# Moving work at the joints of one decoder step: page gathers, operand pieces, squares, splits and closing adds in another order

## The chip, the cores and the metric

The kernel runs on one core of a Trainium2 chip. Times are device microseconds of one execution of the whole program; the time of a kernel is the median of several runs. Five engines work side by side, each through its own queue in order: TensorE (PE, with its weight loads PEld), VectorE (DVE), ScalarE (ACT), GpSimd (POOL), and SyncE (SP), which only issues DMA.

## The reference

One decoder layer in float32, for a prompt of 1024 tokens and 8 sampled tokens with 256 cached positions each; model width 1024, feed-forward width 4096.

```python
z = rmsnorm(x, g_mix) @ w_in          # q, k, v, indexer qi/ki/wi, u, vb, ga, gb
score = sum_h relu(qi_h . ki) * wi_h  # indexer: over the prompt, or over gathered cache pages
idx   = top_k(score, min(256, L//4))  # then softmax attention over the kept keys
o_sgu = u * (tril(w_s) rmsnorm(vb) + b_s)
x = x + (sigmoid(ga) * o_att + sigmoid(gb) * o_sgu) @ w_o
x = x + square(relu(rmsnorm(x, g_ffn) @ w_up)) @ w_down
x = x + sigmoid(rmsnorm(x, g_ple) @ w_pg) * (p @ w_p)
```

For the sampled tokens, keys, values and indexer keys come from paged caches through a page table (8 sequences of 2 pages).

## The kernel before, in words

All activations are feature-major: 8 chunks of 128 features by 1032 tokens (1024 + 8). Each float32 product is made of three passes over a high and a low half of each operand (xh,whi; xl,whi; xh,wlo), so every operand needs a cast to the high half on ACT and a subtraction for the low half on DVE or POOL. `split_weight` does that for a weight chunk (ACT: L195 whi, POOL or DVE: L196 wlo). A projection chunk is 72 matmuls, `acc`.

The program is written out by hand in the order of each engine's queue; there is no scheduler that reorders it. Each engine executes what is emitted for it in that order, and semaphores follow from the data. Generators in a list `paced` are advanced one step at each `tick` of the projection loop; the top-k runs as a background generator on DVE. SBUF tiles called `slot` share a ring of 40 buffers.

In order of time: input norm and indexer queries; projections of queries, keys, values, gates and the spatial gating unit (65 to 690 us of the profiled execution), with the top-k on DVE and the decode path between them; attention to 918; the out-projection w_o, chunks k = 0 to 7, to 1015.7; the up-projection to 1372; a first part of the embedding product p @ w_p to 1393; the down-projection to 1737; the second part to about 1752; w_pg to the end.

- `decode` gathers the indexer's cache pages by 16 indirect DMAs on POOL (L652, tile `kib`); between pairs of them POOL copies decode queries into `zqi` (L684).
- The out-projection also prepares the up-projection's right operand: `scale` (L1309), `square` for the norm (L1248), and `x_piece(i, kk)`, which forms a sum or difference of quarters of x for product i (DVE, in place) and splits it (ACT cast L1317, DVE residual, tile `xop`).
- The up-projection is done by a 7-product scheme on 2 by 2 blocks. 16 steps `USTEPS` of 7 products, each product 24 matmuls into PSUM pairs pa, pd, pc, pb. `up_split` makes the weight pieces (`uop`, L1366). Evictions: `Pair.to` copies on ACT (first, L1292) or adds on DVE. The norm's factor `r` is computed by `inv_rms` in the first step (a power on POOL, L276) and spread over the tokens by transposes (`along_banks`, banks rb and rbd, copied by ACT, L1519 and L1522). At a step's end the two halves `top` and `low` go through relu times norm on DVE and are squared on ACT (L1590, L1595); `operands` then emits the pieces for the down-projection in the next step (`hop`, L1421), partly through DRAM.
- The down-projection has 32 steps (8 passes f over the feed-forward blocks, 4 output pairs o) of 7 products of 12 matmuls. Weight pieces: `down_sums` on POOL (`ds`, L1490 to L1493), `down_hi` on ACT (`dhi`, L1500), `down_lo` on DVE (`dlo`). `split_op` splits the raw operands of products 4 to 6, loaded as `hraw` by `load_op`, in the first step of their pass. In the last pass each step ends with adds of u2 into the result (DVE) and two squares for the next norm (ACT, then sums into `acc` on POOL, L1250).

Of the kernel before, what the change touches and what calls it, by code (L numbers as in the profile page):

```python
# [16 lines left out]
P = 128  # L17
D = 1024
S = 1024
NB = 8  # L20
# [50 lines left out]
def step_kernel(ctx, tc, xT, pT, w_in, w_o, w_up, w_down, w_pg, w_p, gv, gqk, wsT, b_s,  # L71
# [355 lines left out]

    at[0] = 2
# [214 lines left out]
    def decode():  # L643
        pt = small("pt", [P, NB * NPG], I32)
        sp.dma_start(out=pt, in_=bass.AP(tensor=pages.tensor, offset=pages.offset, ap=[[0, P], [1, NB * NPG]]))
        io = small("io", [P, 1], I32)
        pool.iota(io, pattern=[[0, 1]], base=0, channel_multiplier=1)
        pf = small("pf", [P, NB * NPG + 1])
        idx = small("idx", [P, NB * NPG], I32)

        def page(out, cache, j):
            pool.indirect_dma_start(out=out, out_offset=None, in_=cache,  # L652
                                    in_offset=bass.IndirectOffsetOnAxis(ap=idx[:, j:j + 1], axis=0))

# [16 lines left out]
        yield 1  # L671
        yield 1
        dve.tensor_copy(pf[:, :NB * NPG], pt)
        dve.tensor_copy(pf[:, NB * NPG:], io)
        dve.tensor_scalar(idx, pf[:, :NB * NPG], float(P), pf[:, NB * NPG:], op0=ALU.mult, op1=ALU.add)
        kib = slot("kib", [P, NB * NPG, HD])
        zqi = slot("zqi", [64, NB, NB, HI])
        pool.memset(zqi, 0.0)
        for j in range(NB * NPG):
            page(kib[:, j, :], cache_ki, j)  # L680
            if j % 2 == 1:
                for h in range(2):
                    b = j // 2
                    pool.tensor_copy(zqi[:, b, b, h::2], dqi[h * 64:(h + 1) * 64, :, b])  # L684
                yield 1
# [628 lines left out]
    def x_keep(i, kk, r, c):  # L1314
        xop[i, kk] = op = slot("xop", [P, 2, TH], F32R)
        src = quarter(kk, r, c)
        act.copy(op[:, 0], src)  # L1317
        dve.tensor_tensor(out=op[:, 1], in0=src, in1=op[:, 0].bitcast(F32), op=ALU.subtract)

# [3 lines left out]
    def x_piece(i, kk):  # L1323
# [10 lines left out]
        x_keep(i, kk, *((0, 0), (0, 0), (1, 0), (1, 1), (0, 1), (1, 1), (1, 0))[i])  # L1334
# [37 lines left out]
    n1 = Norm(2, "1", x1)  # L1372
    for k in range(KC):
# [10 lines left out]
        if k:  # L1384
            if k < KC - 1:
                scale(k - 1)
            if k - 1 < 4:
                x_piece(0, k - 1)
                x_piece(1, k - 1)
            elif k - 1 == 4:  # L1390
                for i in range(2, 7):
                    x_piece(i, 0)
        if k == KC - 2:
            for g in range(LEAD):
                up_split(g)
            up_load(1)
            scale(k)

# [126 lines left out]
    def up_product(n, i, pair, start, between=None):  # L1525
        w = wop.pop(7 * n + i)
        for kk in range(4):
# [3 lines left out]
            for l, r in ((0, 0), (0, 1), (1, 0)):  # L1531
# [4 lines left out]
    FIRST_X = {1: [(2, 1), (2, 2), (2, 3)], 2: [(3, 1), (3, 2), (3, 3), (4, 1)], 3: [(4, 2), (4, 3)],  # L1536
               4: [(5, 1), (5, 2), (5, 3)], 5: [(6, 1), (6, 2), (6, 3)]}

    for n, (f, j) in enumerate(USTEPS):
# [5 lines left out]
        for i in range(7):  # L1545
# [5 lines left out]
            for x in FIRST_X.get(i, ()) if n == 0 else ():  # L1551
                x_piece(*x)
# [14 lines left out]
            if n == 0 and i == 3:  # L1567
# [9 lines left out]
            if i == 0:  # L1577
                t.to(u, True)
            elif i == 1:
                t.to(c22, True)  # L1580
            elif i == 3:
                for p, o, r in tiles["a"].views(c11, n1.R[:, :TH]):
                    dve.scalar_tensor_tensor(out=o, in0=p, scalar=0.0, in1=r, op0=ALU.max, op1=ALU.mult)
            elif i == 4:
# [7 lines left out]
            elif i == 6:  # L1592
                t.plus(c21, u)
                dve.scalar_tensor_tensor(out=low, in0=low, scalar=0.0, in1=n1.R, op0=ALU.max, op1=ALU.mult)
                act.activation(low, low, AF.Square)  # L1595
# [3 lines left out]
    for low_ in lows:  # L1599
        low_()  # L1600

# [57 lines left out]
    for n, (f, o) in enumerate(steps):  # L1659
# [9 lines left out]
        if o == 2:  # L1669
            for i in range(4, 7):  # L1670
                load_op(follows, i)
# [22 lines left out]
        d.to(c22, first)  # L1694
        if end:
# [3 lines left out]
        split_op(f, 4)  # L1699
# [3 lines left out]
        split_op(f, 5)  # L1703
# [29 lines left out]
        if last:  # L1733
            dve.tensor_tensor(out=d12, in0=d12, in1=u2, op=ALU.add)
            both = acc[:, 2 * o + 1, :].rearrange("p (s c) -> p s c", s=2)
            dve.tensor_tensor(out=both, in0=both, in1=u2.unsqueeze(1).to_broadcast([P, 2, TH]), op=ALU.add)
            for k in (o, o + 4):
                n2.square(k)
            if o == 2:
                embed_load(1)  # L1740
    ks = [0, 4, 1, 5, 2, 6, 3, 7]
# [98 lines left out]
```

## Time and profile before

| | us |
|---|---|
| time, median of 3 runs | 1853.52 (1852.42 to 1854.61) |
| profiled execution, its own time | 1852.57 |
| its span | 1850.6 |
| PE busy | 1771.4 (96%) |
| DVE busy | 1385.2 (75%) |
| ACT busy | 754.7 (41%) |
| POOL busy | 582.9 (31%) |

In rows of a timeline the first number is the start, the second the length; what stands in brackets is the idle time of that engine just before, and what ended it. In rows of waits stand the total, the number of waits and the longest. A line L65 is that of a helper that records every operation of PE and DVE, so those are told apart by the names of their tiles.

### The profile page before, as it was taken

Reading aid. Unit: us, or ns where it says so; the run is one execution under the profiler, and the core shown is the slowest. Engines: PE = TensorE matmul, PEld = TensorE weight load, DVE = VectorE, ACT = ScalarE, POOL = GpSimd, SP = SyncE. Lnnn points to the kernel's source line nnn. Section 1 sums busy time; section 2 is a strip of 40 time slices with the busy share of each in tenths; the row PEclk is TensorE's granted clock in tenths of the full one; section 3 lists DMA queues with packets and bytes.
Section 4 is the critical chain, followed back from the end, with each engine's and each line's share of the span. In section 5 each row is a group of like instructions: output and inputs, shape, how many; then the busy total and the mean of one; then the engine's idle time right before and its main releaser. Section 6 shows DMA issues by size and latency. Waiting matters only on the chain. (4 is left out here: it accounts for less than half of the span.)

```text
span 1850.6 us, 31610 instructions
## 1 busy us (share of the span) xinstructions
PE 1771.4 (96%) x12490; PEld 1657.9 (90%) x12490; DVE 1385.2 (75%) x2505; ACT 754.7 (41%) x1304; POOL 582.9 (31%) x479
## 2 busy tenths in 40 slices
PE   8999988999999999999999899999989999999898
PEld 8998887998999996777698799999989999999798
DVE  7489986989978756777734788888884777777733
ACT  5544332255311136777733543444445322222521
POOL 3233354456323221110013133222323335432321
PEclk9999999999999999999999899999999999999999
DMA  4122132223122264223151154554526566653133
GB/s 172 59 96 103 58 122 85 90 94 114 47 92 69 92 166 119 58 63 98 49 195 69 53 203 180 192 182 175 197 104 230 203 220 236 211 176 127 71 113 122
DMA packets 118932, 236.19 MB, mean 128 GB/s; under 512 B 12856, under 2 KB 57792, under 8 KB 118784
## 3 DMA queue, kind: packets, MB, share of 16 engines
q1 hardware_dynamic: 116592, 229.43, 36.7%
q0 software_dynamic: 2048, 4.72, 0.9%
q8 instruction: 98, 1.61, 0.4%
q14 instruction: 50, 0.41, 0.1%
q10 hardware_dynamic: 144, 0.02, 0.0%
HBM read 155.22 MB, written 78.91 MB: 127 GB/s over the span
## 5 line engine op out<-in xcount | busy, mean ns | idle before, releaser
L65 PE MATMUL acc<-xh,whi 128*128 128x344 f32 (+1 forms) x1144 | 372.8, 329 | 2.2 <-DVE s_q L65 1.8
L65 PE MATMUL acc<-xh,wlo 128*128 128x344 f32 (+1 forms) x1144 | 365.2, 323 | 7.9 <-POOL wlo L196 6.4
L65 PE MATMUL acc<-xl,whi 128*128 128x344 f32 (+1 forms) x1144 | 364.9, 322 | 2.1 <-DVE xl L65 2.1
L65 PEld LDWEIGHTS acc<-xh,whi 128*128 128x128 f32 x1144 | 216.3, 190 | 11.1 <-issue 5.0
L65 PEld LDWEIGHTS acc<-xh,wlo 128*128 128x128 f32 x1144 | 215.9, 189 | 9.1 <-POOL wlo L196 7.0
L65 PEld LDWEIGHTS acc<-xl,whi 128*128 128x128 f32 x1144 | 216.0, 189 | 3.6 <-DVE xl L65 3.1
L65 DVE MATCH_REPLACE8 mask<-m,mask 128x384 f32<-128x384 f32 (+2 forms) x192 | 166.6, 875 | 0.0
L196 POOL TENSOR_TENSOR wlo<-wraw,whi 128x1024 fp32r<-128x1024 f32 x47 | 113.5, 2416 | 159.8 <-ACT whi L195 111.2
L65 DVE MAX8 m<-mask 128x8 f32<-128x384 f32 (+2 forms) x192 | 161.0, 879 | 0.0
L1113 ACT ACTIVATE p<-p,mx,s_q 128x1024 f32<-128x1024 f32 (+7 forms) x128 | 110.4, 864 | 24.2 <-DVE mx L65 23.8
L65 PE MATMUL pa<-xop,uop 128*128 128x258 f32 x768 | 101.3, 289 | 10.9 <-ACT x L1292 10.9
L65 PEld LDWEIGHTS pa<-xop,uop 128*128 128x128 f32 x768 | 96.5, 193 | 14.3 <-ACT x L1292 13.8
L65 PE MATMUL pc<-xop,uop 128*128 128x258 f32 x768 | 101.0, 287 | 2.6 <-ACT xop L1317 1.9
L65 PEld LDWEIGHTS pc<-xop,uop 128*128 128x128 f32 x768 | 96.7, 192 | 4.0 <-ACT xop L1317 2.6
L65 DVE CUSTOM_DVE_ANT_0 p<-sc,mask 128x1024 f32<-128x1024 f32 (+5 forms) x96 | 83.5, 886 | 21.2 <-PE sc L65 20.7
L65 PE MATMUL pd<-xop,uop 128*128 128x258 f32 x768 | 99.2, 285 | 0.0
L65 DVE TENSOR_TENSOR x<-x 128x516 f32<-128x516 f32 x92 | 95.7, 1040 | 0.7
L65 PEld LDWEIGHTS pd<-xop,uop 128*128 128x128 f32 x768 | 96.0, 192 | 0.0
L65 PE MATMUL pc<-hop,dhi 128*128 128x258 f32 x512 | 84.8, 286 | 7.6 <-DVE acc L65 7.6
L65 PE MATMUL sc<-kh,qst 128*128 128x512 f32 (+3 forms) x384 | 89.2, 361 | 1.6 <-DVE mx L65 1.4
L1490 POOL TENSOR_TENSOR ds<-draw 128x256 f32<-128x256 f32 x32 | 31.3, 979 | 186.8 <-DMA draw<-w_down 37.6
L65 PE MATMUL pa<-hop,dhi 128*128 128x258 f32 x512 | 83.4, 285 | 3.7 <-DVE u L65 3.6
(339 smaller groups left out, 4132.7 us busy)
## 6 DMA issues: line engine op xcount, KB each, us to landing
h_d<-hop SPq DMA_DIRECT2D x56, 516.0 KB, 3.7
hop<-h_d SPq DMA_DIRECT2D x56, 516.0 KB, 5.7
wraw<-w_in SPq DMA_DIRECT2D x48, 512.0 KB, 4.7
uraw<-w_up SPq DMA_DIRECT2D x32, 512.0 KB, 4.8
draw<-w_down SPq DMA_DIRECT2D x32, 512.0 KB, 3.7
hs_d<-x SPq DMA_DIRECT2D x42, 258.0 KB, 2.8
hraw<-hs_d SPq DMA_DIRECT2D x21, 516.0 KB, 6.4
q_d<-qs SPq DMA_DIRECT2D x16, 512.0 KB, 3.2
```

Of the source, the lines that this page charges most:

```text
L65: return fn(*args, **kw)
L196: eng.tensor_tensor(out=lo, in0=raws[n], in1=hi.bitcast(F32), op=ALU.subtract)
L1113: eng.activation(s, s, AF.Exp, bias=env["mx"][:, 4 + h:5 + h], scale=sc, accum_out=env["sum"][:, h:h + 1])
L1490: pool.tensor_tensor(out=s_[:, 0], in0=a21, in1=a22, op=ALU.add)
```

## The change

It moves operations; each of them is still done once and with the same operands.

- Index pages: the page table's DMA, the index computation and the 16 gathers move from `decode` into a generator `index_pages`, paced through the indexer-query stage. In `decode` only the zqi copies remain.
- Out-projection: pieces go into a list `xq` and are issued two after each eviction of a block, so that a chunk's whi and wlo come ahead of them. Four pieces of products 2 and 3 come into the last chunk.
- First up step: pieces come in batches (`x_pieces`: all sums, then all casts, then all residuals). The transposes of the norm's factor move from product 3 to product 4, and the eviction that uses it from product 3's end to product 4's.
- Up steps: the square of `low` is kept in `squared` and issued after the next step's copy out of pa.
- End of up: the loads for the first embedding come at product 2, its casts at product 4, its residuals at products 4, 5 and 6, and the first sums of down weights at product 6.
- Down: `split_op` of raw operand 4 comes in step o = 2 and of 5 in o = 3 of the pass before, only 6 stays in o = 0; the raw loads come one per step.
- Last pass: the closing adds and squares of a step become `close`, called after product 1 of the next step.

```diff
+    def index_pages():
+        sp.dma_start(out=pt, in_=bass.AP(tensor=pages.tensor, offset=pages.offset, ap=[[0, P], [1, NB * NPG]]))
+        pool.iota(io, pattern=[[0, 1]], base=0, channel_multiplier=1)
+        yield 1
+        dve.tensor_copy(pf[:, :NB * NPG], pt)
+        dve.tensor_copy(pf[:, NB * NPG:], io)
+        dve.tensor_scalar(idx, pf[:, :NB * NPG], float(P), pf[:, NB * NPG:], op0=ALU.mult, op1=ALU.add)
+        yield 1
+        paged["kib"] = kib = slot("kib", [P, NB * NPG, HD])
+        for j in range(NB * NPG):
+            page(kib[:, j, :], cache_ki, j)
+            if j % 2 == 1:
+                yield 1
...
+    paced.append(pages_)
...
-        for j in range(NB * NPG):
-            page(kib[:, j, :], cache_ki, j)
-            if j % 2 == 1:
-                for h in range(2):
-                    b = j // 2
-                    pool.tensor_copy(zqi[:, b, b, h::2], dqi[h * 64:(h + 1) * 64, :, b])
-                yield 1
+        yield 1
+        for b in range(NB):
+            for h in range(2):
+                pool.tensor_copy(zqi[:, b, b, h::2], dqi[h * 64:(h + 1) * 64, :, b])
+            yield 1
...
+    def x_pieces(which):
+
+        for i, kk in which:
+            x_sum(i, kk)
+        for i, kk in which:
+            xop[i, kk] = op = slot("xop", [P, 2, TH], F32R)
+            act.copy(op[:, 0], quarter(kk, *AT[i]))
+        for i, kk in which:
+            less(xop[i, kk][:, 1], quarter(kk, *AT[i]), xop[i, kk][:, 0].bitcast(F32))
...
-        for a, b, p in (in_step(M, W=W0 if k == 0 else None) if k in (0, KC - 1) else dense(M)):
+        blocks = in_step(M, W=W0 if k == 0 else None) if k in (0, KC - 1) else dense(M)
+        while xq and k == KC - 1:
+            x_pieces([xq.pop(0)])
+        for a, b, p in blocks:
             dve.tensor_tensor(out=x1[k][:, a:b], in0=p, in1=x1[k][:, a:b], op=ALU.add)
+            for _ in range(2):
+                if xq and k > 1:
+                    x_pieces([xq.pop(0)])
...
             if k - 1 < 4:
-                x_piece(0, k - 1)
-                x_piece(1, k - 1)
+                xq += [(0, k - 1), (1, k - 1)]
             elif k - 1 == 4:
-                for i in range(2, 7):
-                    x_piece(i, 0)
+                xq += [(i, 0) for i in range(2, 7)]
+            elif k - 1 == 5:
+                xq += [(2, 1), (3, 1)]
         if k == KC - 2:
...
             scale(k)
+            xq += [(2, 2), (3, 2)]
...
-    FIRST_X = {1: [(2, 1), (2, 2), (2, 3)], 2: [(3, 1), (3, 2), (3, 3), (4, 1)], 3: [(4, 2), (4, 3)],
-               4: [(5, 1), (5, 2), (5, 3)], 5: [(6, 1), (6, 2), (6, 3)]}
+    FIRST_X = {1: [(2, 3), (3, 3)], 2: [(4, 1), (4, 2)], 3: [(4, 3), (5, 1)],
+               4: [(5, 2), (5, 3), (6, 1)], 5: [(6, 2), (6, 3)]}
+    squared = []
...
+            if end and i == 2:
+                embed_load(0)
             if end and i == 3:
-                embed_load(0)
                 down_load(0)
                 down_load(1)
-            if end and i == 5:
+            if end and i == 4:
                 lows, first_embed = embed(0)
+            if end and i > 3:
+                lows.pop(0)()
+            if end and i == 6:
                 down_sums(0)
...
-            if n == 0 and i == 3:
+            if n == 0 and i == 4:
                 def between():
                     n1.R = along_banks(n1.r, "R_1")
...
             if i == 0:
                 t.to(u, True)
+                if squared:
+                    x = squared.pop()
+                    act.activation(x, x, AF.Square)
...
-            elif i == 3:
+            if i == (4 if n == 0 else 3):
                 for p, o, r in tiles["a"].views(c11, n1.R[:, :TH]):
...
-                act.activation(low, low, AF.Square)
+                if end:
+                    act.activation(low, low, AF.Square)
+                else:
+                    squared.append(low)
...
-    for low_ in lows:
-        low_()
...
-        if o == 2:
-            for i in range(4, 7):
-                load_op(follows, i)
+        if o:
+            load_op(follows, o + 3)
...
         d.to(c22, first)
+        if last and o:
+            close()
...
-        split_op(f, 4)
         product(n, f, 2, A12, a, False)
         a.to(c11, first)
         free(2)
-        split_op(f, 5)
+        if o > 1:
+            split_op(follows, o + 2)
...
         if last:
-            dve.tensor_tensor(out=d12, in0=d12, in1=u2, op=ALU.add)
...
+            def close(o=o, d12=d12, u2=u2):
+                dve.tensor_tensor(out=d12, in0=d12, in1=u2, op=ALU.add)
...
             if o == 2:
                 embed_load(1)
+    close()
```

Three places show what stands where in a queue. The first is POOL. Before, in the decode path: `kib` are the pages, `zqi` the decode queries, `sg` a gate, `wlo` the low half of a projection's weight.

```order
L652 DMA kib<-cache_ki,idx 128x64 x2
L684 COPY zqi<-dqi 64x4 x2
L839 TENSOR_SCALAR sg<-sg 128x1032
L196 TENSOR_TENSOR wlo<-wraw,whi 128x1024
L652 DMA kib<-cache_ki,idx 128x64 x2
L684 COPY zqi<-dqi 64x4 x2
L481 AFFINE_SELECT mask<-mask 128x128
```

Now, in the indexer-query stage (`r_x` is the input norm's factor, raised to its power on POOL):

```order
L196 TENSOR_TENSOR wlo<-wraw,whi 128x1024
L436 DMA kib<-cache_ki,idx 128x64 x2
L276 TENSOR_TENSOR r_x<-r_x,half 128x9
L436 DMA kib<-cache_ki,idx 128x64 x2
L196 TENSOR_TENSOR wlo<-wraw,whi 128x1024
L436 DMA kib<-cache_ki,idx 128x64 x2
L409 COPY kid<-kis 64x8
L436 DMA kib<-cache_ki,idx 128x64 x2
L196 TENSOR_TENSOR wlo<-wraw,whi 128x1024
L436 DMA kib<-cache_ki,idx 128x64 x6
L196 TENSOR_TENSOR wlo<-wraw,whi 128x1024
L436 DMA kib<-cache_ki,idx 128x64 x2
```

The gathers have left the neighbourhood of the gates' weights and stand among the weights of the indexer's queries.

The second place is ACT at the end of the out-projection, from chunk 6 to chunk 7: `sq` is the norm's square, `xop` the operand pieces, `whi` the high half of chunk 7's weight. Before:

```order
L1248 ACTIVATE sq<-x_9370 128x1032
L1309 ACTIVATE x_9370<-x_9370,gvt 128x1032
L1317 CAST xop<-x_9370 128x516 x5
L195 CAST whi<-wraw 128x1024
L1248 ACTIVATE sq<-x_9370 128x1032
```

Now:

```order
L1259 ACTIVATE sq<-x_9370 128x1032
L1320 ACTIVATE x_9370<-x_9370,gvt 128x1032
L195 CAST whi<-wraw 128x1024
L1334 CAST xop<-x_9370 128x516 x5
L1259 ACTIVATE sq<-x_9370 128x1032
```

The weight's cast has passed the five pieces.

The third is ACT at the joint of two up steps: the squares are the ACTIVATE rows (first the top half, then the low half), the COPY empties pa. Before:

```order
L1590 ACTIVATE x_9370<-x_9370 128x1032
L1366 CAST uop<-uraw 128x512
L1595 ACTIVATE x_9370<-x_9370 128x1032
L1366 CAST uop<-us 128x512
L1292 COPY x_9370<-pa 128x516
```

Now:

```order
L1621 ACTIVATE x_9370<-x_9370 128x1032
L1381 CAST uop<-uraw 128x512
L1381 CAST uop<-us 128x512
L1303 COPY x_9370<-pa 128x516
L1609 ACTIVATE x_9370<-x_9370 128x1032
```

The low half's square has passed a weight cast and the copy.

More of the change, by code (lines that the diff above doesn't have):

```diff
@@ L426, in index_weights, with page @@
                           in1=r2w[:NB, NT:].to_broadcast([NB, HI]), op=ALU.mult)
+    paged = {}
+    pt = small("pt", [P, NB * NPG], I32)
+    io = small("io", [P, 1], I32)
+    pf = small("pf", [P, NB * NPG + 1])
+    idx = small("idx", [P, NB * NPG], I32)
+    def page(out, cache, j):
+        pool.indirect_dma_start(out=out, out_offset=None, in_=cache,
+                                in_offset=bass.IndirectOffsetOnAxis(ap=idx[:, j:j + 1], axis=0))
+    def index_pages():
[11 more added lines that the diff above has]
+                yield 1
+    pages_ = index_pages()
     at[0] = 2
@@ L643, in decode @@
     def decode():
[L644 to L653, printed above, removed]
+        while pages_ in paced:
+            yield 1
         sel = small("sel", [64, NB, HQ])
@@ L670, in decode @@
         sp.dma_start(out=wc, in_=wd.rearrange("b (h o) -> (b h) o", o=1))
-        yield 1
[L672 to L676, printed above, removed]
+        kib = paged["kib"]
         zqi = slot("zqi", [64, NB, NB, HI])
         pool.memset(zqi, 0.0)
-        for j in range(NB * NPG):
-            page(kib[:, j, :], cache_ki, j)
-            if j % 2 == 1:
-                for h in range(2):
-                    b = j // 2
-                    pool.tensor_copy(zqi[:, b, b, h::2], dqi[h * 64:(h + 1) * 64, :, b])
-                yield 1
+        yield 1
+        for b in range(NB):
+            for h in range(2):
+                pool.tensor_copy(zqi[:, b, b, h::2], dqi[h * 64:(h + 1) * 64, :, b])
+            yield 1
         yield 1
@@ L1312, in quarter, with x_sum @@
         return xg[kk + 4 * r][:, c * TH:c * TH + TH]
[L1314 to L1318, printed above, removed]
     def less(out, x, y):
         dve.tensor_tensor(out=out, in0=x, in1=y, op=ALU.subtract)
-    def x_piece(i, kk):
+    def x_pieces(which):
[6 more added lines that the diff above has]
+            less(xop[i, kk][:, 1], quarter(kk, *AT[i]), xop[i, kk][:, 0].bitcast(F32))
+    AT = ((0, 0), (0, 0), (1, 0), (1, 1), (0, 1), (1, 1), (1, 0))
+    def x_sum(i, kk):
         b11, b12, b21, b22 = (quarter(kk, r, c) if i > 1 or not r else None for r in range(2) for c in range(2))
@@ L1333, in x_piece @@
             less(b21, b21, b22)
-        x_keep(i, kk, *((0, 0), (0, 0), (1, 0), (1, 1), (0, 1), (1, 1), (1, 0))[i])
     wraws, wsum, wop = {}, {}, {}
@@ L1372, in step_kernel @@
     n1 = Norm(2, "1", x1)
+    xq = []
     for k in range(KC):
@@ L1550, in step_kernel @@
             up_split(7 * n + i + LEAD)
-            for x in FIRST_X.get(i, ()) if n == 0 else ():
-                x_piece(*x)
+            if n == 0 and i in FIRST_X:
+                x_pieces(FIRST_X[i])
             if i:
@@ L1578, in step_kernel @@
                 t.to(u, True)
+                if squared:
+                    x = squared.pop()
+                    act.activation(x, x, AF.Square)
             elif i == 1:
                 t.to(c22, True)
-            elif i == 3:
+            if i == (4 if n == 0 else 3):
                 for p, o, r in tiles["a"].views(c11, n1.R[:, :TH]):
                     dve.scalar_tensor_tensor(out=o, in0=p, scalar=0.0, in1=r, op0=ALU.max, op1=ALU.mult)
-            elif i == 4:
+            if i == 4:
                 t.to(c22, False)
@@ L1733, in step_kernel @@
         if last:
-            dve.tensor_tensor(out=d12, in0=d12, in1=u2, op=ALU.add)
[L1735 to L1738, printed above, removed]
+            def close(o=o, d12=d12, u2=u2):
+                dve.tensor_tensor(out=d12, in0=d12, in1=u2, op=ALU.add)
+                both = acc[:, 2 * o + 1, :].rearrange("p (s c) -> p s c", s=2)
+                dve.tensor_tensor(out=both, in0=both, in1=u2.unsqueeze(1).to_broadcast([P, 2, TH]), op=ALU.add)
+                for k in (o, o + 4):
+                    n2.square(k)
             if o == 2:
                 embed_load(1)
+    close()
     ks = [0, 4, 1, 5, 2, 6, 3, 7]
```

## The prediction

> **What bounds the kernel now.** I read the page's busy table first, then the waits of TensorE, then the windows of the stages, and then the timeline around each long wait.
>
> ```profile
> span 1850.6 us, 31610 instructions
> PE 1771.4 (96%) x12490; PEld 1657.9 (90%) x12490; DVE 1385.2 (75%) x2505; ACT 754.7 (41%) x1304; POOL 582.9 (31%) x479
> ```
>
> TensorE (PE) is busy for all but 79.2 us. No matmul is added or removed, so the change can win only those idle microseconds, plus what the clock loses after them. The waits of PE over the whole span, as total, times and longest:
>
> ```profile
> PE pa L65 <- ACT x L1292: 10.9, 14, 0.8
> PE pc L65 <- DVE acc L65: 7.6, 8, 1.0
> PE acc L65 <- POOL wlo L196: 6.4, 2, 6.1
> PE acc L65 <- DVE pl L65: 5.3, 1, 5.3
> PE vtr L65 <- ACT rl L470: 4.4, 2, 4.1
> PE rb L65 <- POOL r L276: 4.2, 1, 4.2
> PE pa L65 <- DVE u L65: 3.6, 3, 1.8
> PE acc L65 <- ACT whi L195: 2.9, 1, 2.9
> PE pc L65 <- ACT xop L1317: 1.9, 3, 1.0
> PE acc L65 <- DVE pwlo L65: 1.6, 1, 1.6
> PE pd L65 <- DVE dlo L65: 0.5, 1, 0.5
> ```
>
> Nearly every row is a joint that the diff touches. The windows show the stages: after the length come busy time and instructions of PE, PEld, DVE, ACT and POOL, then the granted clock.
>
> ```profile
> 918.00:992.00 74.00, 74.00 (x471) 74.00 (x472) 31.85 (x41) 25.48 (x29) 14.53 (x7) 1.00 0.42 151
> 1000.36:1015.70 15.34, 14.31 (x72) 13.80 (x73) 5.20 (x8) 4.72 (x6) 4.05 (x3) 0.78 0.30 104
> 1015.70:1050.90 35.20, 28.42 (x191) 25.82 (x190) 25.63 (x42) 16.55 (x29) 8.64 (x5) 0.86 0.12 45
> 1050.90:1350.50 299.60, 289.50 (x2363) 286.80 (x2363) 254.36 (x367) 128.14 (x211) 92.06 (x56) 0.99 0.51 183
> 1350.50:1393.00 42.50, 33.74 (x233) 32.54 (x233) 32.62 (x45) 22.56 (x39) 7.93 (x8) 0.92 0.23 88
> 1393.00:1693.00 300.00, 293.27 (x2408) 290.99 (x2407) 208.90 (x336) 87.45 (x108) 115.24 (x120) 1.00 0.59 207
> 1693.00:1752.00 59.00, 51.63 (x356) 47.16 (x355) 46.57 (x65) 27.29 (x34) 22.52 (x15) 0.97 0.18 65
> 296.00:690.00 394.00, 391.64 (x2555) 378.03 (x2554) 327.50 (x572) 118.12 (x226) 149.91 (x102) 1.00 0.31 95
> 290.80:294.00 3.20, 3.16 (x12) 3.16 (x13) 0.00 (x0) 0.78 (x1) 2.15 (x3) 0.53 0.56 179
> ```
>
> An undisturbed stretch (918 to 992) does 471 instructions in 74.00 us, 0.157 us each. A wait costs twice: itself, and a clock near one half for the next microseconds (last row, right after the 6.1 us wait).
>
> **The change, part by part.** The sum is made against this execution: its own time is 1852.57 us (span 1850.6 and 2.0 around it), 0.95 below the median of 1853.52, which I use as base.
>
> *A, index pages.* Sixteen page gathers and their zqi copies stand in POOL's queue in decode, ahead of a wlo that PE wants:
>
> ```profile
> 278.38 0.18 POOL L684 COPY zqi<-dqi 64x4 f32<-64x4 f32 x1 [3.10 <-DMA kib<-cache_ki,idx]
> 288.44 2.34 POOL L196 TENSOR_TENSOR wlo<-wraw,whi 128x1024 fp32r<-128x1024 f32 x1
> 290.84 0.66 PE L65 MATMUL acc<-xh,wlo 128*128 128x344 f32 x1 [6.14 <-POOL wlo L196]
> ```
>
> A zqi copy waits for a transfer (3.10), and POOL holds everything behind it. With the gathers gone this wlo can start some 10 us earlier (eight zqi pairs and twelve gathers stand in the stretch before it), so the wait goes whole (6.1) and with it the slow clock: 3.2 us at 0.53, half of it lost, 1.5. That is 7.6. The cost lies in the query stage, where the gathers now stand between POOL's operations of 42 to 80 us, with one small DMA more on SP and three small operations on DVE:
>
> ```profile
> L652 POOL DMA_INDIRECT kib<-cache_ki,idx x16 | 18.1, 1129 | 4.9 <-issue 2.8 <-POOL zqi L684 1.8
> 65.05 2.39 POOL L196 TENSOR_TENSOR wlo<-wraw,whi 128x1024 fp32r<-128x1024 f32 x1 [5.33 <-ACT whi L195]
> 77.77 2.40 POOL L196 TENSOR_TENSOR wlo<-wraw,whi 128x1024 fp32r<-128x1024 f32 x1 [10.33 <-ACT whi L195]
> ```
>
> They take 18.1 us in all, 1.13 each. POOL's gaps ahead of its wlo are 5.33 and 10.33 us, filled by waiting for ACT's whi: two to four gathers (2.3 to 4.5) go into the one and six (6.8) into the other, so they cost nothing. If the indices came late, the wlo of these rows would queue behind them. I take 7; bounds 4 (a later wait by VectorE eats some) and 7.6. The vtr wait of 4.1 I leave as it is: ahead of it POOL is held by a power for fk, not by a gather.
>
> *B, end of the out-projection.* On ACT five piece casts, each waiting for a DVE subtraction, stand ahead of the last block's whi:
>
> ```profile
> 998.74 0.62 ACT L1317 CAST xop<-x 128x516 fp32r<-128x516 f32 x1 [1.43 <-DVE x L65]
> 999.27 1.04 ACT L195 CAST whi<-wraw 128x1024 fp32r<-128x1024 f32 x1
> ```
>
> PE waits 2.9 for it (the row from ACT whi); then 72 matmuls take 15.34 us instead of 72 x 0.157 = 11.3, at clock 0.78. With whi ahead both go: 2.9 + 4.0 = 6.9. The pieces now fall into the block itself, where DVE has 5.20 of 15.34 us busy. I take 6.5; bounds 4 and 7.
>
> The Trainium skill ("TensorE: Matmul & The Clock Gate", Part 1) says that the clock halves after at least one idle window of about 3.4 us. This trace shows 0.78 after a wait of 2.9 followed by shorter ones, so the measurement decides here; by the page alone part B would be worth the waits only, about 4, and the whole forecast some 3 us less.
>
> *C, first up step.* It lasts 35.20 us for 191 instructions of PE. In the steps after it one takes 289.50 / 2363 = 0.1225, so 23.4 would do. Waits are 4.2 (rb, for POOL's power) and 1.9 for xop, and most of the rest is the clock at 0.86. DVE works 25.63 of it, and between a piece's subtraction and its residual it idles for ACT's cast:
>
> ```profile
> 1027.52 0.70 DVE L65 TENSOR_TENSOR xop<-x,xop 128x516 fp32r<-128x516 f32 x1 [0.69 <-ACT xop L1317]
> ```
>
> The batches close that 0.69, some twelve times, and four pieces have moved into B. So DVE's 25.6 us become the floor: 35.2 - 25.6 = 9.6 at best. The transposes move one product (24 x 0.1225 = 2.9 us) later, which takes most of the 4.2; but now rbd waits until ACT has copied the first rb, and ACT's queue has the batch's casts of products 4 and 5 ahead of that copy, which wait for DVE. I charge 1.6 for it: gain 8; bounds 4 (the stall as long as the rb wait was) and 9.6.
>
> *D, the square behind the copy.* In each of 14 steps ACT squares the previous step's low half, then casts, then copies u out of pa, for which PE waits:
>
> ```profile
> 1141.30 1.07 ACT L1595 ACTIVATE x<-x 128x1032 f32<-128x1032 f32 x1 [2.70 <-DVE x L65]
> 1142.78 0.58 ACT L1292 COPY x<-pa 128x516 f32<-128x516 f32 x1
> 1143.41 3.15 PE L65 MATMUL pa<-xop,uop 128*128 128x258 f32 x24 [0.75 <-ACT x L1292]
> ```
>
> Behind the copy, the 1.07 us square is after what PE waits for. The copy may start 1 us earlier, more than the 0.75 of the wait. All 10.9 go unless another wait follows in its place; DVE is busy 254 of 299.6 us there, so a little may. I take 10; bounds 7 and 10.9. Who waits for the square is the hop cast of a later product, with ACT 128 of 299.6 busy.
>
> *E, end of up.* Embedding casts and residuals move one product earlier, each residual between products. The 5.3 and 1.6 for pl and pwlo are what can go, and the clock behind them (stage at 0.92); but DVE has 32.62 us of work in 42.50, and pl only moves ahead of work which is late itself, up to the hop pieces that bound the embedding. I take 3; bounds 0 and 6.9.
>
> *F, raw splits.* Of three hop splits in one down step, two move to the step before. Here a 1.23 us split stands just ahead of the eviction for which PE waits:
>
> ```profile
> 1441.50 1.23 DVE L65 TENSOR_TENSOR hop<-hraw,hop 128x1032 fp32r<-128x1032 f32 x1
> 1442.64 0.75 DVE L65 TENSOR_TENSOR acc<-pc,acc 128x258 f32<-128x258 f32 x2
> ```
>
> One such wait of about 0.95 occurs per pass, 7.6 in 8. One split stays in that step; with two gone, DVE's queue is 2.4 us shorter. I take 4.5; bounds 2 and 7. The loads move to one a step on SP, far ahead of their use.
>
> *G, closing adds of the last pass.* They move behind product 1 of the next step, after the pd eviction. This removes the 3.6 for u, the 0.5 for dlo, and some 1.5 of slow clock (as in A). But the squares follow the adds, and POOL's sums of the next step's weight halves stand behind the squares:
>
> ```profile
> 1712.75 4.92 POOL L1250 TENSOR_TENSOR acc<-acc,sq 128x1032 f32<-128x1032 f32 x2 [4.85 <-ACT sq L1248]
> 1717.62 1.47 POOL L1490 TENSOR_TENSOR ds<-draw 128x256 f32<-128x256 f32 x1
> 1719.16 0.74 POOL L1491 TENSOR_TENSOR ds<-ds,draw 128x256 f32<-128x256 f32 x1
> 1721.32 1.05 ACT L1500 CAST dhi<-ds 128x1024 fp32r<-128x1024 f32 x1 [6.78 <-POOL ds L1493]
> ```
>
> Before, this dhi comes just in time for product 1 of the last step. Now the closing adds start two products and an eviction later (2 x 12 x 0.122 + 0.7 = 3.6), and squares, sums and dhi with them. I count dhi 3 us late in the last step and 2 in the one before, where there is more room, dlo 0.8 more in each: 6.6, with 1.5 of slow clock. 5.6 gained against 8.1: I take -2; bounds -5 (four more sums of 0.74 that take twice as long, as one does above) and +3 (dhi late by half of that).
>
> The Trainium skill ("GPSIMD Engine Reference", Key points) says that GpSimd shares its SBUF interfaces with VectorE, with contention when a DVE instruction has two SBUF inputs. The trace agrees: one ds sum took 1.47 and the next 0.74. If the rule held for all eight sums of the two steps, G would cost 8 x 0.73 = 5.8 more and the sum would be 31.
>
> Sum: 7 + 6.5 + 8 + 10 + 3 + 4.5 - 2 = 37, so 1853.5 - 37 = 1816.5.
>
> **The rivals.** *Half of it comes back.* DVE has 25.6 us in C, 32.6 in E and 46.6 of 59 in the tail, so it may be the next bound at each joint; then the lower bounds hold for C, E, F and G (4, 0, 2, -5) and A, B, D give 6, 5, 9: 21, so 1832. For it speaks the DVE column; against it, that most waits are one operation in the wrong place in a queue.
>
> *The upper bounds.* A 7.5, B 7, C 9.6, D 10.9, E 6, F 6.5, G +2: 49.5, so 1804. For it speaks that no work is added; against it, that each engine must fall in with the others at every joint.
>
> *The square's move does nothing.* If ACT's queue ahead of the copy is what delays it (the uop cast, which waits on POOL's us), D gives 2 and the rest stands: 1824.5. Against it: the square's own start, with 2.70 of idle before it, shows ACT waiting just for the low half.
>
> *Slower: the pages hold a buffer.* The kib tile is one of 40 ring buffers and now stays in use from the query stage to the end of decode, while all other tiles turn over in the remaining 39. If a tile then waits for its buffer, ACT's rl or a weight load comes late, as in the vtr row: 4.1 and 1.5 of clock a time. The other parts give 30, so it decides from 6 such waits on; ten would give 1880. The window from 296 to 690 us speaks against so many: PE idles 2.4 us there in all.
>
> **How the numbers follow.** Forecast (1808 to 1825, D's rival apart) 0.60; half comes back 0.17; the square does nothing 0.07; upper bounds 0.10; slower 0.04; a remainder of 0.02 near no change. The range leaves out the far ends: 1804 to 1832. About 0.2% is what a measurement of this kernel can tell from no change, so faster is 0.93, same 0.03, slower 0.04.
>
> **What would show it.** A: no PE wait for wlo near 290, gathers among POOL's wlo at 45 to 80. B: whi ahead of the pieces and a last block of 11 to 12 us. C: the first up step under 30 us with the rb wait under 1. D: the row pa from ACT gone. E: the pl wait shrunk. F: pc from DVE acc under 3 in all. G: a new wait of pd for dhi of 2 to 3 us in the last two steps. I would be wrong if gathers sat in front of a wlo that PE awaits, if the rb copies stalled behind casts by over 4 us, or if waits by VectorE took the place of those removed.

## The result

The changed kernel takes 1822.65 us (median of 4 runs, 1820.57 to 1824.43) against 1853.43 before in the same comparison: ratio 0.9833, interval 0.9816 to 0.985. The forecast was 1816.5 in a range of 1804 to 1832. The profiled execution after has a span of 1822.1 us, 28.5 less than before. Its page begins:

```profile
span 1822.1 us, 31615 instructions
PE 1765.3 (97%) x12490; PEld 1655.0 (91%) x12490; DVE 1396.8 (77%) x2505; ACT 754.5 (41%) x1304; POOL 589.4 (32%) x479
```

PE's longest waits (total, times, longest):

```profile
PE pc L65 <- DVE acc L65: 7.3, 11, 1.5
PE acc L65 <- DVE pwlo L65: 5.9, 2, 5.1
PE rbd L65 <- ACT R L1542: 5.4, 1, 5.4
...
PE pd L65 <- ACT dhi L1523: 2.7, 2, 2.5
...
PE rb L65 <- POOL r L276: 1.1, 1, 1.1
```

The row of pa waiting for ACT's copy (10.9) is gone, as are wlo at 6.1, whi at 2.9, pl at 5.3 and u at 3.6. Three rows are new in kind or size: rbd 5.4, pwlo 5.1, dhi 2.5. The row pc from DVE acc has not shrunk: 7.3 in 11 waits, formerly 7.6 in 8.

Apart from the transposes into rb, which stand one product later, PE runs the same products in the same order in both kernels. So the start of a product in both timelines shows how far ahead the changed kernel is at each place, and what each part gave:

| place (time before, us) | ahead by | what this part gave | forecast |
|---|---|---|---|
| before the last chunk of the out-projection (985) | 6.65 | A, pages: 6.65 | 7 |
| first product of up (1015.72) | 13.75 | B, whi ahead: 7.1 | 6.5 |
| third up step (1072.90) | 18.28 | C, first step: 3.0 in it, 1.5 behind it | 8 |
| last up step (1349.35) | 31.28 | D, square, 13 of 14 joints: 13.0 | 10 for 14 |
| first down step (1392.92) | 33.14 | last joint of D 1.0, E 0.9 | 3 for E |
| last three down steps (1697.87) | 32.66 | F, splits: -0.5 | 4.5 |
| end of the span (1850.6) | 28.5 | G, closing adds: -4.2 | -2 |

The 1.5 behind C's step is clock, not the square: before, the granted clock is 0.56 from 1050.88 to 1055.57, at the start of the second step, and in the changed kernel it is 1.00 at that place. The kernel with the square alone (below) keeps that slow start: its second step takes 22.15, before 22.02, the changed kernel's 20.50.

B has no run of its own. In the changed kernel's trace the wait for whi is gone and the last chunk takes 11.35, where it took 15.36. Of those 4.0 about 1.0 was a second wait (acc for DVE's x, 1.0) and the rest clock, which was 0.50 from 1000.35 to 1007.18 and 1.00 from there on. All eleven kernels here that have this part win 7.1 at this place.

In the first up step the new wait stands in the chain of two queues. ScalarE and one operation of VectorE in the timeline after:

```profile
1019.96 1.75 DVE L65 TENSOR_TENSOR xg<-xg,x 128x516 f32<-128x516 f32 x1
1020.07 0.62 ACT L1334 CAST xop<-x 128x516 fp32r<-128x516 f32 x1 [2.52 <-DVE x L65]
1021.80 0.62 ACT L1334 CAST xop<-xg 128x516 fp32r<-128x516 f32 x1 [1.11 <-DVE xg L65]
1023.42 0.62 ACT L1334 CAST xop<-x 128x516 fp32r<-128x516 f32 x1 [1.00 <-DVE x L65]
1023.95 1.07 ACT L1542 COPY R<-rb 128x512 f32<-128x512 f32 x2
```

The eight transposes into rb are done at about 1019, but the copy that empties rb starts at 1023.95, behind three casts that wait for VectorE (2.52, 1.11, 1.00). What VectorE does for them are three subtractions that run from 1018.28 to 1023.38 and take 1.75 or 1.76 each, where 0.68 is usual. Three sums of GpSimd for the next weights run beside them, from 1018.02 to 1022.84; the first two are:

```profile
1018.02 1.46 POOL L1370 TENSOR_TENSOR us<-uraw 128x512 f32<-128x512 f32 x1
1019.56 1.60 POOL L1371 TENSOR_TENSOR us<-us,uraw 128x512 f32<-128x512 f32 x1
```

At 0.68 each, the three would be over 3.2 us earlier. No run moves those sums, so how much of the 5.4 that would save is not shown. The stages after, as windows with the columns of those before (the granted clock stands ahead of the last two):

```profile
1001.97:1034.12 32.15, 25.00 (x191) 23.88 (x189) 27.66 (x43) 14.14 (x25) 9.67 (x5) 0.89 0.14 49
1034.12:1318.07 283.95, 283.95 (x2355) 283.75 (x2354) 251.76 (x365) 128.57 (x210) 92.01 (x56) 1.00 0.54 193
1318.07:1359.78 41.71, 35.28 (x242) 34.34 (x241) 33.78 (x47) 23.07 (x38) 7.75 (x8) 0.92 0.26 89
1359.78:1665.21 305.43, 300.08 (x2438) 295.48 (x2437) 220.20 (x344) 87.46 (x108) 118.75 (x120) 1.00 0.58 204
1665.21:1724.00 58.79, 49.18 (x328) 44.00 (x326) 44.87 (x58) 27.96 (x36) 23.24 (x15) 0.97 0.19 65
```

The up steps after the first have no idle microsecond left (283.95 of 283.95). The first up step, the end of up and the last down steps still have.

### The profile page after: what moved, and what is told of

It reads as the page before. It is cut to its first block, busy times and chain, and to the rows that moved or that the text cites. A ratio compares the mean times of both kernels' runs of the same rounds, so it can differ in the third digit from the quotient of the medians.

```text
span 1822.1 us, 31615 instructions
## 1 busy us (share of the span) xinstructions
PE 1765.3 (97%) x12490; PEld 1655.0 (91%) x12490; DVE 1396.8 (77%) x2505; ACT 754.5 (41%) x1304; POOL 589.4 (32%) x479
## 3 DMA queue, kind: packets, MB, share of 16 engines
HBM read 155.22 MB, written 78.91 MB: 128 GB/s over the span
## 4 chain that ended last, share of the span: by engine, by line
PE 74%; DVE 12%; issue 5%; ACT 3%; POOL 3%; DMA 1%; another core or an unknown queue 0%; SPq 0%; DVEq 0%; POOLq 0%; ACTq 0%
PE acc L65 30%; PE pa L65 9%; PE pd L65 9%; PE pc L65 8%; PE po L65 4%; PE pb L65 4%; PE pp L65 4%; PE sc L65 3%; DVE mask L65 3%; DVE m L65 2%; DVE x L65 1%; DVE dlo L65 1%; POOL wlo L196 1%; PE mix L65 1%; DVE qs L65 1%
## 5 line engine op out<-in xcount | busy, mean ns | idle before, releaser
L1197 POOL TENSOR_TENSOR m<-g,ms 128x256 f32<-128x256 f32 x32 | 23.5, 733 | 195.6 <-DVE mx L65 95.2
```

The lines of the kernel that those rows point to most:

```text
L1197: eng.tensor_tensor(out=m[:, 2 * c:2 * c + 2, cols], in0=env["g2"], in1=env["ms"], op=ALU.add)
```

## The experiments

Each was compared with the kernel before on the same chip, and the kernel before came out between 1852.03 and 1853.52 in these comparisons. So two kernels of the table are compared by the last column, the distance to before in the same comparison, and what a part gave is read from product starts on PE as above.

| kernel | us | ratio to before, interval | us below before |
|---|---|---|---|
| changed kernel | 1822.65 | 0.9833, 0.9816 to 0.985 | 30.8 |
| square alone on before | 1838.23 | 0.992, 0.9904 to 0.9937 | 13.8 |
| pages alone on before | 1845.0 | 0.9949, 0.9933 to 0.9966 | 8.5 |
| copies of R ahead of casts | 1819.89 | 0.982, 0.9804 to 0.9836 | 33.5 |
| closing adds back | 1817.93 | 0.9809, 0.9792 to 0.9825 | 35.5 |
| splits back | 1822.61 | 0.9831, 0.9814 to 0.9847 | 30.8 |
| embedding back | 1822.09 | 0.9833, 0.9817 to 0.985 | 31.3 |
| embedding earlier | 1825.08 | 0.9851, 0.9835 to 0.9867 | 27.0 |
| x1's load first | 1819.42 | 0.982, 0.9803 to 0.9836 | 32.6 |
| three mended | 1813.64 | 0.9791, 0.9775 to 0.9807 | 38.4 |
| dlo behind pc's eviction | 1818.06 | 0.9804, 0.9788 to 0.982 | 35.5 |
| four mended | 1809.7 | 0.9757, 0.974 to 0.9773 | 43.8 |
| four mended, sums first | 1805.88 | 0.9743, 0.9729 to 0.9756 | 47.1 |

**Square alone (part D).** The kernel before with only this:

```diff
                 t.to(u, True)
+                if squared:
+                    x = squared.pop()
+                    act.activation(x, x, AF.Square)
...
-                act.activation(low, low, AF.Square)
+                if end:
+                    act.activation(low, low, AF.Square)
+                else:
+                    squared.append(low)
```

> The kernel before with one part of the change alone: in the up steps the square of the low half stands behind the next copy out of pa. Theory (a wait of 0.78 costs PE about 1.02, since the matmuls right after it also run late): 14 joints x 1.02 = 14.3 us; time 1838 to 1840.5. Rival 1 (a wait costs its own length): 10.9 us; time 1842 to 1843.5. Rival 2 (VectorE takes over as the bound in these steps): under 8 us; time above 1845.

Measured: 1838.23, 13.8 less than the 1852.03 of before in that comparison; the span is 14.3 less. So a wait of 0.78 cost 1.02. The product starts show where the rest went: in a step of the kernel before, product 1 with the wait behind it takes 3.80 us and product 2 takes 2.99, where the others take 2.89; one step takes 21.27 before and 20.26 after. Without a wait a product starts some 0.16 before the recorded end of the one ahead of it; a recorded wait begins only at that end, so this lead is lost on top of it. No other wait took the place. D's term was too small because it priced the wait at its recorded length.

**Pages alone (part A).** The kernel before with `index_pages` and the shortened `decode` of the diff.

> The kernel before with one part of the change alone: the index pages gathered in the query stage. Theory (the gathers and the zqi copies that wait for them hold POOL's queue in decode and nothing is late for them earlier): the wait for wlo near 290 us (6.1) goes with its slow clock; 6.5 to 7.6 us; time 1844.5 to 1847. Rival (part of it comes back later in the projections, where VectorE is 95% busy): 3 to 5 us; time 1848 to 1850.

Measured: 1845.0, 8.5 less than 1853.52; PE is 8.0 ahead at the first up product. At the old place of the wait PE goes from 0.3 behind to 7.4 ahead, 7.7 in all (in the changed kernel from 0.6 behind to 7.1 ahead), which is the forecast wait and its clock. What stands at 985 us lies between 6.6 and 8.7 in the kernels with this part, so one such reading is good to about 1 us. In the query stage GpSimd has room for all of it:

```profile
46.77 1.21 POOL L436 DMA_INDIRECT kib<-cache_ki,idx  x1 [0.66 <-DVE idx L65]
48.28 0.95 POOL L436 DMA_INDIRECT kib<-cache_ki,idx  x1 [0.30 <-issue]
49.48 1.84 POOL L276 TENSOR_TENSOR r_x<-r_x,half 128x9 f32<-128x9 f32 x1 [0.25 <-issue]
...
66.09 2.42 POOL L196 TENSOR_TENSOR wlo<-wraw,whi 128x1024 fp32r<-128x1024 f32 x1 [2.46 <-ACT whi L195]
```

Every wlo still waits for ScalarE's whi, not for a gather (the one behind six gathers starts at 78.91, 0.14 after its whi is done). Only the power for r_x comes right behind two gathers, 0.25 after them, and nothing waits for it. The vtr wait stayed (3.6), as forecast; the rival of a missing buffer did not show.

**Copies of R ahead of the casts (part C).**

```diff
-            if n == 0 and i in FIRST_X:
-                x_pieces(FIRST_X[i])
+            if n == 0 and i == 4:
+                for piece in FIRST_X[i]:
+                    x_sum(*piece)
+            elif n == 0 and i in FIRST_X:
+                x_pieces(FIRST_X[i])
...
             up_product(n, i, t, i in (0, 1, 4, 5), between)
+            if n == 0 and i == 4:
+                x_split(FIRST_X[i])
```

(`x_split` is the second and third loop of `x_pieces`.)

> Changed kernel, with the three casts of product 5 and 6 pieces in the first up step moved on ScalarE behind the copies of the norm's factor out of rb. Theory (the transposes stall because ACT's copy stands behind casts that wait for VectorE): the 5.4 us wait of rbd falls under 0.5, product 5 then waits 1 to 2 us for its own pieces, the first up step gets 4 to 6 us shorter; time 1817 to 1819. Rival (VectorE's work is the floor of this step): the wait comes back at product 5 in nearly full length, step shorter by less than 1.5; time 1821 to 1823.

Measured: 1819.89. PE's waits in that stretch:

```profile
PE pb L65 <- DVE xop L65: 1.1, 1, 1.1
PE rb L65 <- POOL r L276: 1.1, 1, 1.1
PE pc L65 <- DVE x L65: 0.7, 1, 0.7
...
PE rbd L65 <- ACT R L1544: 0.2, 1, 0.2
```

And its window of the first up step:

```profile
1001.20:1030.78 29.58, 25.41 (x190) 23.38 (x189) 26.89 (x41) 14.25 (x25) 9.73 (x5) 0.94 0.15 54
```

The wait for rbd falls from 5.4 to 0.2, so its cause is shown. But the step gets only 2.6 shorter (32.15 to 29.58), 1.9 of which remain at the first down step: products 5 and 6 now wait for their pieces. VectorE works 26.89 of the 29.58 us, and its three subtractions still take 1.75 to 1.80 each. Both theories were half right (the one said 4 to 6, the other under 1.5): the place in the queue costs some 2 us, and behind it stands VectorE's work, as part C's best case of 25.6 had it.

**Closing adds back (part G).** `close` is called at the end of its own step, as before the change.

> Changed kernel, with the closing adds and squares of the last pass back at the end of their own step. Theory (late squares hold POOL's sums, so dhi comes late): the waits for dhi (2.5) and behind it go, the waits of pa for u (0.3, 1.5, 1.8) come back; the last three down steps get 2 to 4 us shorter; time 1818.5 to 1821. Rival (the two orders cost the same, the loss lies in VectorE's amount of work there): no change within 0.7 us; time 1822 to 1823.5.

Measured: 1817.93. PE is 1.6 ahead of the changed kernel at down step 29 (steps are counted from 0) and 5.8 ahead in the second embedding: the deferral cost 4.2. The longest waits between 1660 and 1735 us, first of the changed kernel, then with the adds back:

```profile
PE pc L65 <- DVE acc L65: 2.8, 3, 1.5
PE pd L65 <- ACT dhi L1523: 2.7, 2, 2.5
PE acc L65 <- ACT e L1493: 2.4, 9, 1.0
PE pd L65 <- DVE dlo L65: 1.0, 2, 0.5
PE acc L65 <- DVE pwlo L65: 0.8, 1, 0.8
```

```profile
PE pa L65 <- DVE u L65: 3.7, 3, 1.8
PE acc L65 <- ACT e L1493: 2.4, 9, 1.0
PE pd L65 <- DVE dlo L65: 0.5, 1, 0.5
PE pc L65 <- DVE acc L65: 0.3, 1, 0.3
```

The waits for u (3.7) had gone as forecast, and dhi came late, as forecast, but by less: 2.5 in the last step and 0.2 in the one before, where 3 and 2 were counted. Not forecast was the row pc, 2.8 against 0.3: the closing adds on VectorE also delay the evictions of their new step.

**Splits back (part F).** The three splits and raw loads where they were.

> Changed kernel, with the three raw splits back in the first step of their pass and the three raw loads back in step 2. Theory (a split costs PE about as much where it now stands, and the load or split in step 2 meets POOL's add of x1 and a slow residual): the 0.95 wait per pass comes back, the waits of 1.0 and 1.4 in passes 3 and 4 go; the down stage changes by less than 1.5 us; time 1821 to 1824. Rival (spreading is worth the forecast 4.5 and something else ate it): 1826 to 1828.

Measured: 1822.61, no change (0.9 us of PE's lead lost over the down stage): spreading was worth next to nothing, where 4.5 was forecast. The steps of one pass show why. In microseconds, for steps 1 to 4 of the down stage (step 4 is the first of a pass): 10.13, 10.12, 10.12, 11.46 before; 10.12, 10.38, 10.35, 10.83 after. The 1.3 at one step became 0.25, 0.25 and 0.7 at three. And in steps 12 to 19, where GpSimd adds x1, the eight steps took 85.41 before and 87.49 after. Not all of these 2.1 come from the spreading: with the splits back they take 86.94, and over the kernels here the old order took 85.4 to 86.9 and the spread one 85.7 to 87.9. In the other 21 steps the gain is small but clear: 219.2 to 219.5 with the old order, 217.8 to 218.0 with the spread one. VectorE and GpSimd in step 14 after:

```profile
1510.36 1.22 DVE L65 TENSOR_TENSOR hop<-hraw,hop 128x1032 fp32r<-128x1032 f32 x1
1511.50 0.69 DVE L65 TENSOR_TENSOR acc<-pd,acc 128x516 f32<-128x516 f32 x1
1512.11 2.58 DVE L65 TENSOR_TENSOR dlo<-draw,dhi 128x768 fp32r<-128x768 f32 x1
1514.61 0.75 DVE L65 TENSOR_TENSOR acc<-pc,acc 128x258 f32<-128x258 f32 x2
1511.29 2.58 POOL L1762 TENSOR_TENSOR acc<-acc,xr 128x1032 f32<-128x1032 f32 x1 [2.49 <-DMA xr<-x_d]
```

The split has pushed the residual dlo (0.95 when alone) into GpSimd's add, where it takes 2.58, and the eviction of pc that PE waits for stands behind it. The eviction of pd (1511.50), one of whose inputs is PE's bank in PSUM, keeps its 0.69 beside the same add.

**x1's load first.** In the down loop the block of `add_x1` (with its DMA) stands ahead of the calls of `load_op`.

> Changed kernel, with the load of x1's chunk in down steps 12 to 19 issued ahead of the step's operand loads on SP instead of behind them. Theory (the load comes late behind the raw operand, so POOL's add runs against the residual dlo on VectorE and stretches it): the add starts about 2 us earlier in steps 14 and 18, dlo takes 1.0 us again and not 2.6 to 3.0, steps 14, 16 and 18 get 2 to 3.5 us shorter in all; time 1819 to 1821. Rival (wherever the add runs in these steps it stretches some two-input operation of VectorE, now the split itself): steps 14 and 18 stay above 11.3 us; time 1822 to 1823.5.

Measured: 1819.42. In step 14 the add now starts at 1506.59 instead of 1511.29, 2.2 earlier counted from the start of its step, and dlo takes 0.94. Steps 12 to 19 take 85.63 instead of 87.49. But the add stretches the split now:

```profile
1506.59 2.43 POOL L1762 TENSOR_TENSOR acc<-acc,xr 128x1032 f32<-128x1032 f32 x1 [0.25 <-DMA xr<-x_d]
1507.90 2.21 DVE L65 TENSOR_TENSOR hop<-hraw,hop 128x1032 fp32r<-128x1032 f32 x1
```

Steps 14 and 18 stand at 10.95 and 11.12, where steps at the same place of other passes take 10.1 to 10.4, and step 16 got longer (12.20 for 11.83). So the three steps are 1.2 shorter in all, not 2 to 3.5: the add moved as the theory said, and the rival's mechanism took its place. Nor is the 1.9 of the eight steps clear of chance: with the old order of the load, the kernel with the embedding back takes 85.71 there. By the last column of the table it gains 1.8 on the changed kernel; but PE is 1.8 ahead of that kernel when the down stage starts, and nothing up to there is touched by this edit: so much a single profile varies. What this edit is worth stays open.

**dlo behind pc's eviction.**

```diff
-        down_lo(n + 1, 0)
         down_hi(n + 1, 1)
...
         c.to(c22, False)
+        down_lo(n + 1, 0)
```

> Changed kernel, with the residual dlo of the next step's A pieces on VectorE one place later in each down step: behind the first eviction of pc instead of ahead of it. Theory (PE waits for that eviction, which stands behind the raw split and dlo; moving the splits only shared this out): the waits of pc for acc (7.3 in 11) fall under 2; steps with a split go from 10.37, 10.56 and 10.83 to about 10.15 to 10.4, and a dlo stretched by POOL's add no longer costs anything in steps 14, 16, 18; down stage 6 to 10 us shorter; time 1813 to 1817. Rival (VectorE's queue as a whole is late, the eviction of pb or the next dlo is waited for instead): less than 3 us; time 1820 to 1822.5.

Measured: 1818.06, above the theory's range, though the down stage is 6.1 shorter, as the theory said. Of PE's waits between 1358 and 1660 us this is left, and no wait for pc's eviction (4.8 in 9 in the same stretch of the changed kernel):

```profile
PE pd L65 <- DVE dlo L65: 1.7, 3, 0.7
PE pa L65 <- DVE dlo L65: 0.3, 1, 0.3
```

Outside steps 12 to 19 all steps fall to 10.1 or 10.2, also those with a split (before the change 11.46), and 29 steps take 299.31 instead of 305.43. In steps 12 to 19 little is won (86.73 for 87.49): 12, 13, 16 and 17 still take 11.1 to 11.4, because a dlo stretched by the add now comes late for its own product. The theory had ruled that out for 14, 16 and 18. The cause of F's waits outside those steps is shown: the eviction stood behind dlo, and the split only pushed dlo. Behind step 29, 0.7 is lost again in G, whose waits for dhi grew from 2.7 to 4.8.

**Embedding back, embedding earlier (part E).** Once everything where it was before; once earlier still, the load by five products, the casts by three, the residuals by two:

```diff
-            if end and i == 2:
+            if n == len(USTEPS) - 2 and i == 4:
                 embed_load(0)
...
-            if end and i == 4:
+            if end and i == 1:
                 lows, first_embed = embed(0)
-            if end and i > 3:
+            if end and 1 < i < 5:
                 lows.pop(0)()
```

> Changed kernel, with loads, casts, residuals and first sums of the first embedding back where they were before. Theory (the embedding is bounded by the pieces of low's square, which the earlier residuals delay; little is won): the stretch from the last up step to the first down step gets 0.5 to 1.5 us longer; time 1823 to 1824.5. Rival (moving the residuals is worth the forecast 3 us or more): 1825.5 to 1827.

> Changed kernel, with loads, casts and residuals of the first embedding earlier: load in up step 14, casts at product 1 and residuals at products 2, 3 and 4 of the last step. Theory (pwlo waits 5.1 because VectorE's queue at products 5 and 6 is full): that wait falls under 1, low's square comes 2 us earlier, the stretch gets 2 to 4 us shorter; time 1819 to 1821. Rival (VectorE is full through the whole last step, so that the residuals only push its evictions): change under 0.7 or slower; time 1822 to 1825.

Measured: back, the stretch from the last up step to the first down step takes 42.60 instead of 41.71, 0.9 longer; the median does not tell it (1822.09). Earlier, it takes 44.64, 2.9 longer, and the kernel 1825.08, 3.8 closer to before than the changed kernel. The longest waits there, of the changed kernel and of the earlier one:

```profile
PE acc L65 <- DVE pwlo L65: 5.1, 1, 5.1
PE acc L65 <- ACT e L1493: 1.3, 2, 1.1
```

```profile
PE acc L65 <- ACT e L1493: 4.8, 4, 1.4
PE pc L65 <- DVE x L65: 3.2, 1, 3.2
```

The wait for pwlo is gone, and its work now delays an eviction by 3.2 and ScalarE's e by 4.8: the rival holds. VectorE works 33.8 of 41.7 us here, and in both orders what was moved only changed who is late.

**Three mended; four mended.** Copies of R ahead, closing adds back, x1's load first; then dlo behind pc's eviction as well.

> Changed kernel with three parts mended at once: casts behind the copies of the norm's factor, closing adds back in their own step, load of x1's chunk ahead of the operand loads. Theory (the three places are apart in time and add up: 1.9 + 4.2 + 1.5): time 1813.5 to 1816.5. Rival (what one place gains the next one waits for): 1817 to 1819.

> The kernel with three parts mended, and the residual dlo behind the eviction of pc. Theory (the places add up; the early load of x1 is then worth nothing more, since dlo no longer stands in the way): three mended minus 5 to 8; time 1805.5 to 1809. Rival (VectorE's queue as a whole): 1811 to 1814.

Measured: 1813.64 and 1809.7. The three add up (by their distances to before, 7.6 below the changed kernel; 1.9 + 4.2 + 1.9 = 8.0 were read from the parts). The fourth gives 5.4 counted so, 3.9 between the medians, and 4.7 in the 29 steps, at the lower edge of the 5 to 8 expected: the split steps outside 12 to 19 are at 10.1, but the steps with an early add of x1 are not (11.09 to 11.43 in steps 12, 14, 16 and 18). That the load of x1 would be worth less now, or cost something, was not tried apart.

**Four mended, but sums first (part G again).** Deferred closing adds, behind the sums and the first weight cast:

```diff
-        if last and o:
-            close()
         if end:
             lows.pop(0)()
         down_sums(n + 1)
         down_hi(n + 1, 0)
+        if last and o:
+            close()
```

> The kernel with four parts mended, but with the closing adds deferred as in the change, only behind the next weight halves' sums in POOL's queue and the first weight cast on ScalarE, not ahead of them. Theory (what the deferral lost came from the sums standing behind the squares; deferring itself saves the waits of pa for u): no wait for dhi above 0.5 in the last two steps, the three waits for u (4.1 with their slow clock) gone; 3 to 5 us below the kernel with four parts mended: 1805 to 1807.5. Rival (the closing work is late for something else wherever it is deferred to, the final squares and the second embedding): within 1 us of that kernel or slower: 1809 to 1812.

Measured: 1805.88 (1803.68 to 1807.18), the fastest of all. PE's waits from 1640 to 1735 us, with four mended and with the sums first:

```profile
PE pa L65 <- DVE u L65: 4.1, 3, 1.8
PE acc L65 <- ACT e L1495: 2.4, 9, 1.0
PE pd L65 <- DVE dlo L65: 0.5, 1, 0.5
```

```profile
PE acc L65 <- ACT e L1495: 2.0, 7, 1.0
PE pc L65 <- DVE acc L65: 1.5, 1, 1.5
PE pa L65 <- DVE dlo L65: 0.4, 1, 0.4
```

Neither u nor dhi is waited for. The span is 4.4 shorter, of which 3.3 arise from down step 29 on. So deferring was right, and its place ahead of the sums was what cost.

## Why the prediction came out as it did

The time lies in the range, 6.15 above the forecast; the sign and the order of size were right. That it came so close is in part luck. By the table of product starts D brought 4 more than its term, while C, E, F and G together brought 12.8 less (3.5, 2.1, 5.0 and 2.2); without what D's term had missed, the time would have been some 10 above the forecast.

- *A and B* were sized well (7 and 6.5; 6.65 and 7.1 in the changed kernel). Both rest on one operation that stood in the wrong place of a queue, with an idle engine at its new place. In B, 1.0 of what the prediction put down to the clock was a second wait; the sum is the same. B shows a slow clock behind a wait of 2.9 as well. The Trainium skill's rule of a whole idle window ("TensorE: Matmul & The Clock Gate", Part 1) would have priced B at 4, and the 7.1 speaks for the trace's row.
- *C* gave 4.5 of its 8. It named the mechanism, a stall of rbd behind casts that wait for VectorE, and charged 1.6 for it; the wait was 5.4. I had casts waiting for VectorE in view, but not that each waits anew for its own subtraction: three waits of 1.0 to 2.5 in a row, while GpSimd's sums run beside those subtractions (1.75 in the row shown, where 0.68 is usual). I used this stretching in G, on GpSimd's side, and left it out here. With the stall mended VectorE is the floor.
- *D* was too small by 4: the step that failed is the price of a wait. "The copy may start 1 us earlier, more than the 0.75 of the wait" was right, but PE gains 1.02 a joint: the recorded wait leaves out the lost lead of the next product (0.16) and its slower run (0.10).
- *E* failed in "The 5.3 and 1.6 for pl and pwlo are what can go": pl's wait went and pwlo's grew to 5.1. The rival *half of it comes back*, with 0 for E, was nearer.
- *F* failed in "with two gone, DVE's queue is 2.4 us shorter". What was late was one eviction, behind dlo and one split. Each step that received a split got the same queue and a quarter of the old loss, and the step that lost two still had one. And I took GpSimd's add of x1 not into account at all; the steps with it lost 2.1 against the profile before, of which some 0.5 goes with the splits' place in the one comparison that moves only them (86.94 and 87.49).
- *G* had its mechanism right (dhi 2.5 late in the last step) and was too mild by 2: the waits for dhi are 2.7 in all where 5 was counted, but the closing adds also stand ahead of evictions (pc, 2.8 in three waits), which had no term.
- The rival *the square's move does nothing* fell, and so did *the pages hold a buffer*: the whole stretch to 985 us is faster.

The tell-tales I gave were right for A, B, D and G, and showed C and F wrong: first up step 32.15 instead of under 30, pc from acc 7.3 instead of under 3. E's was badly chosen: the wait for pl went, as it said, and E still failed. Two of the three signs of being wrong came: the rb copies stalled for 5.4, over the 4 named, and VectorE's pwlo took the place of its pl. The x1 collision stays open in one point: step 18 took 12.02 and 11.77 in two kernels and about 10.15 in three others with the same order there, so when the transfer lands varies from run to run.

## What to carry to other kernels

Moving an operation pays when its old place stands ahead of something awaited and its new place has an idle engine; look at the new place's queue for who waits behind it there (R's copies behind casts, sums behind squares, an eviction behind dlo). An eviction that the bounding engine waits for belongs ahead of every preparation for the next step on its engine: one line of order made 29 steps 6.1 shorter here, spreading the preparation next to nothing. On an engine that is busy for most of a stretch (VectorE 81% at the end of up), moved work may only change which of its users is late.

## What the runs showed of the hardware

A wait of PE cost more than its recorded length: 0.78 recorded, 1.02 lost, with the granted clock at 1.00. In the joint at 1141 of the kernel before, 0.75 is recorded. The product then starts without the lead of some 0.16 that others have over the recorded end of the one ahead, and it runs 3.15 where 3.05 is usual.

Behind some waits the granted clock was 0.50 for 3.4, 6.8 or 10.2 us and then 1.00 again: for 6.83 behind the 2.9 for whi before, and for 3.41 behind a wait of 1.55 (1512.05, closing adds back). Waits of up to 1.4 in the same stage of the changed kernel had no such stretch behind them (clock 1.00).

And VectorE's operation with both inputs in SBUF takes up to three times as long while GpSimd adds two tiles: dlo 0.95 alone, 2.58 beside the add; a split 1.22 and 2.21. In both rows it ends 0.8 to 1.1 after the add does, nearly its own length, as though it did most of its work only when the add was over. The Trainium skill states this sharing of SBUF interfaces ("GPSIMD Engine Reference", Key points) without a size; the runs here agree and give one.
